# A hybrid decoder step: token scales of the first blocks taken from rows, dt's projection in small PSUM tiles, a second weight tile that lags, and a passage whose scalings are asked for in four parts

## The chip, the core and the metric

The kernel runs on one core of a Trainium2 chip: TensorE (PE; its weight loads are PEld), VectorE (DVE), ScalarE (ACT), GpSimd (POOL) and SyncE (SP), which here only starts DMAs. Each engine runs its own list of instructions in order; semaphores join them. The metric is the device time of one execution in microseconds (us). Before the change it was 2792.21 us, the median of three runs (2789.77 to 2793.71).

## The reference, cut to what matters

A trunk of two layers runs over 1104 token rows: 64 sample tokens, 16 learned meta tokens and 1024 prompt tokens, of 1024 features each. Layer 0 is a Mamba-2 mixer and a feed-forward block, layer 1 a sliding-window attention and a feed-forward block. The change touches only the way into layer 0:

```python
def _rmsnorm(x, g):
    xf = x.astype(jnp.float32)
    r = lax.rsqrt(jnp.mean(xf * xf, axis=-1, keepdims=True) + EPS)
    return (xf * r).astype(x.dtype) * g

def _mamba2_mixer(u, ...):              # u = _rmsnorm(h, ssm_norm_g)
    zxbcdt = u @ w_in                   # 2048 z, 3072 x/B/C, 32 dt columns
    z, xbc, dt_raw = ...
    ...                                 # conv of 4 taps over xbc, silu
    dt = jax.nn.softplus(dt_raw + dt_bias)
    a = dt * (-jnp.exp(a_log))
    y, h_new = _ssd_chunked(...)        # chunks of 128 tokens
    out = _gated_group_rmsnorm(y + xs * d_skip, z, gate_g) @ w_out
```

So each token needs one scale, the root of its mean square, before any column of `w_in` can be applied to it.

## The kernel before

Tokens stand in two halves: 592 (the 64 sample and 16 meta tokens, the block of 80, and four blocks of 128) and 512 (four blocks of 128). In SBUF the features lie on the partitions: `hA` holds the first half as 8 feature tiles of 128 by 592. A product keeps float32 accuracy by three passes of a faster format: weight and token operands are split into a high and a low part (`wH`, `wL`, `uH`, `uL`), and each 128-feature tile takes wH·uH, wH·uL and wL·uH (lines L75 to L77 in `mm3`). ScalarE casts the high part (L138 for weights), VectorE or GpSimd subtracts to get the low part (L149). `ws` holds a raw weight as it was loaded, 128 by 1024; both parts are then stored to DRAM (`kept`, L152) for the second half. Only two buffers each of `ws`, `wH` and `wL` exist.

**The opening** is `input_first`, written out by hand for the first two weight tiles (B and C of group 0). The first half is cut at token 336 (`at[0]`, `at[1]`): the first part is blocks 0 to 2, the second blocks 3 and 4. For the first part the square of each feature tile is taken (L345, L347), and one-column matmuls against ones add it over the features (L350), so the sums come out with tokens on the partitions. `roots` is one power on GpSimd (L356), `diagonal` writes the scales on a diagonal (L361), and `spread` multiplies it by ones (L368), which puts each token's scale on all partitions. Then `scaled` (L372), `high` (L375) and `low` (L378) make the operands tile by tile, and `dense` (L385) runs the products, both weight tiles for each feature tile. For blocks 3 and 4 rows of tokens are loaded instead, and ScalarE squares and sums each in one instruction (L403). `warm` (L337) runs matmuls of ones whose result is not used. `in_order` chains the instructions of this part on TensorE, VectorE, ScalarE and GpSimd in the order of the list.

After it, `xbc` projects the other tiles of group 0; `conv` (L647 to L668) reads each accumulator out of PSUM with two ScalarE copies and runs the taps on VectorE (`cc`, L664). `dt_proj` (L485) is the projection to dt in full float32, from the unscaled tokens, with the gain folded into its weight `wdt` by GpSimd (L436); its result is copied to `dtraw` (L490), and the token's scale is applied later in `dt_tables`. `acc` names the large accumulators of PSUM (two in the first half, three in the second), `ps` the small ones (four and five). A group's `ssd` takes a chunk at a time; group by group the sample tokens are decoded (`decode`, matmul L811, operand `decs`), and each chunk needs a table of decays, `E`, broadcast from DRAM by SP (L601).

**The passage** (`boundary`) joins the halves: the last out-projections of the first half run while `input_second` reads, scales (L471) and splits the second half's tokens. A string of letters gives the order of the parts, and `in_order` holds it on TensorE.

Outside these places the program's own scheduler sets the order on every engine, by priorities and its own idea of times, before the program runs.

## Time and profile before

| | |
|---|---|
| median of three runs | 2792.21 us |
| the profiled execution | 2798.55 us, its span 2796.7 us |
| mean granted TensorE clock | 0.985 |
| TensorE busy | 2723.8 us (97%) |
| VectorE, ScalarE, GpSimd busy | 1988.1, 1193.6, 525.2 us |
| first product matmul (L385) | at 17.13 us |
| first matmul after the opening (L75) | at 38.06 us |

In rows in order of time, the first number is the start in us, the second the busy time; `out<-in` are the program's tiles, `xN` is the count of instructions, and the bracket holds how long the engine was idle before and what ended that. A matmul's time includes its way through the array, so neighbours overlap; the distance of two starts is the cost of one. The granted clock is the share of TensorE's full clock that it was given.

### The profile page before, as it was taken

What the parts mean: (1) busy time and instruction counts of PE and PEld (TensorE: products, weight loads), DVE (VectorE), ACT (ScalarE), POOL (GpSimd) and SP (SyncE); (2) the same over time, 40 slices, a digit from 0 to 9 for tenths busy, and PEclk for the clock granted to TensorE, in tenths of its full rate; (3) what the DMA queues carried; (4) which work ended last, traced back from release to release, by engine and by line L of the source; (5) the groups of instructions that cost most, each with busy time, mean ns of one, the idle gap of its engine ahead of it and who ended that gap; (6) DMA issues with size and microseconds to landing.
All of it is one profiled execution on the core that took longest, in us unless ns stands there. A gap on an engine that the chain in (4) does not pass through costs nothing.

```text
span 2796.7 us, 50176 instructions
## 1 busy us (share of the span) xinstructions
PE 2723.8 (97%) x19649; PEld 2515.4 (90%) x19649; DVE 1988.1 (71%) x3401; ACT 1193.6 (43%) x2491; POOL 525.2 (19%) x740
## 2 busy tenths in 40 slices
PE   9899999999999999999999999999999999999998
PEld 8788999887888899999999997676989999999998
DVE  7677666666564898778779881556479777877886
ACT  4656554356441443334342142555444333334224
POOL 2565545315322100000000002433220000000000
PEclk9999999999999999999999999999999999999999
DMA  7766767566554344334378652011714443438764
GB/s 267 246 218 218 270 225 246 210 232 203 190 189 155 121 145 164 139 123 166 130 291 286 235 190 81 27 44 29 215 59 153 153 142 122 166 136 293 275 217 160
DMA packets 261713, 498.60 MB, mean 178 GB/s; under 512 B 23652, under 2 KB 140004, under 8 KB 261476
## 3 DMA queue, kind: packets, MB, share of 16 engines
q1 hardware_dynamic: 257748, 488.49, 50.9%
q10 hardware_dynamic: 3728, 6.90, 0.7%
q8 instruction: 155, 2.54, 0.4%
q14 instruction: 82, 0.67, 0.1%
HBM read 320.01 MB, written 175.30 MB: 177 GB/s over the span
## 4 chain that ended last, share of the span: by engine, by line
PE 84%; DVE 8%; ACT 2%; DMA 2%; issue 1%; POOL 1%; SPq 0%; POOLq 0%; DVEq 0%; ACTq 0%
PE wacc L1589 10%; PE wacc L1591 10%; PE wacc L1590 10%; PE acc L75 6%; PE acc L76 6%; PE acc L77 6%; PE dacc L1589 5%; PE dacc L1590 5%; PE dacc L1591 5%; PE pP L75 2%; PE pP L76 2%; PE pP L77 2%; PE ps L746 1%; PE ps L749 1%; DVE cc L664 1%
## 5 line engine op out<-in xcount | busy, mean ns | idle before, releaser
L1245 ACT CAST wo<-ws 128x512 fp32r<-128x512 f32 x428 | 263.3, 620 | 537.6 <-PE wacc L1590 250.3
L1589 PE MATMUL dacc<-bo,wo 128*128 128x276 f32 (+1 forms) x1232 | 355.5, 289 | 4.8 <-ACT sumX L1777 2.1
L1590 PE MATMUL dacc<-bo,wo 128*128 128x276 f32 (+1 forms) x1232 | 356.0, 289 | 0.0
L1591 PE MATMUL dacc<-bo,wo 128*128 128x276 f32 (+1 forms) x1232 | 355.2, 289 | 0.0
L1246 DVE TENSOR_TENSOR wo<-ws,wo 128x512 fp32r<-128x512 f32 x428 | 296.3, 696 | 49.6 <-ACT wo L1245 38.7
L75 PE MATMUL acc<-uH,wH 128*128 128x336 f32 (+2 forms) x808 | 267.6, 331 | 2.6 <-ACT wH L138 2.2
L77 PE MATMUL acc<-uH,wL 128*128 128x336 f32 (+2 forms) x808 | 266.4, 330 | 1.2 <-DVE wL L149 1.2
L76 PE MATMUL acc<-uL,wH 128*128 128x336 f32 (+2 forms) x808 | 266.6, 330 | 0.0
L1589 PEld LDWEIGHTS dacc<-bo,wo 128*128 128x128 f32 x1232 | 232.6, 189 | 5.6 <-ACT sumX L1777 2.3
L1590 PEld LDWEIGHTS dacc<-bo,wo 128*128 128x128 f32 x1232 | 231.9, 188 | 0.0
L1591 PEld LDWEIGHTS dacc<-bo,wo 128*128 128x128 f32 x1232 | 231.8, 188 | 0.0
L75 PEld LDWEIGHTS acc<-uH,wH 128*128 128x128 f32 x808 | 154.1, 191 | 18.2 <-issue 4.9
L77 PEld LDWEIGHTS acc<-uH,wL 128*128 128x128 f32 x808 | 153.7, 190 | 13.2 <-issue 3.1
L76 PEld LDWEIGHTS acc<-uL,wH 128*128 128x128 f32 x808 | 153.6, 190 | 12.5 <-issue 3.9
L664 DVE SCALAR_TENSOR_TENSOR cc<-raw,vectors_sb,cc 128x616 f32<-128x616 f32 (+1 forms) x144 | 135.1, 945 | 41.1 <-ACT cc L662 39.5
L2442 POOL MEMSET mask<- 128x64 f32 x1 | 0.2, 151 | 715.0 <-PE dacc L1591 715.0
L75 PE MATMUL acc<-yH,wH 128*128 128x336 f32 (+1 forms) x360 | 122.9, 342 | 9.2 <-DVE hA L917 3.7
L77 PE MATMUL acc<-yH,wL 128*128 128x336 f32 (+1 forms) x360 | 121.0, 336 | 0.5 <-DMA wL<-kept 0.5
L76 PE MATMUL acc<-yL,wH 128*128 128x336 f32 (+1 forms) x360 | 120.9, 336 | 0.5 <-DVE yL L82 0.5
L1765 DVE TENSOR_TENSOR hN<-hN,dacc 128x552 f32<-128x552 f32 (+1 forms) x132 | 94.3, 718 | 19.8 <-PE dacc L1591 19.2
L1589 PE MATMUL wacc<-N4H,wo 128*128 128x276 f32 (+1 forms) x352 | 103.0, 293 | 5.3 <-DVE hA L1602 2.4
L1589 PE MATMUL wacc<-B11H,wo 128*128 128x276 f32 (+1 forms) x352 | 103.4, 294 | 3.0 <-DVE big L917 3.0
(569 smaller groups left out, 8502.7 us busy)
## 6 DMA issues: line engine op xcount, KB each, us to landing
kept<-wH SPq DMA_DIRECT2D x56, 512.0 KB, 3.2
kept<-wL SPq DMA_DIRECT2D x56, 512.0 KB, 3.4
ws<-ffn_w_gate SPq DMA_DIRECT2D x44, 512.0 KB, 4.1
ws<-ffn_w_up SPq DMA_DIRECT2D x44, 512.0 KB, 4.5
ws<-ffn_w_down SPq DMA_DIRECT2D x44, 512.0 KB, 5.8
ws<-ssm_w_in SPq DMA_DIRECT2D x40, 512.0 KB, 5.2
wH<-kept SPq DMA_DIRECT2D x38, 512.0 KB, 3.4
wL<-kept SPq DMA_DIRECT2D x38, 512.0 KB, 4.4
```

Source lines behind the costliest of these rows:

```text
L75: nc.tensor.matmul(out, wH, xH, start=start, stop=False)
L76: nc.tensor.matmul(out, wH, xL, start=False, stop=False)
L77: nc.tensor.matmul(out, wL, xH, start=False, stop=stop)
L664: nc.vector.scalar_tensor_tensor(o, raw[:, k : k + n], w(k), o, ALU.mult, ALU.add)
L746: nc.tensor.matmul(pyv[64 * q : 64 * q + 64, t, :], xd[:n, t, q, :], Ev[:, 4 * q + t, :], start=True, stop=True)
L749: nc.tensor.matmul(pst[:], bt[lo:n], xw[lo:n].rearrange("p t q d -> p (t q d)"), start=True, stop=True)
L1245: nc.scalar.copy(H, src)
L1246: (low or nc.vector).tensor_tensor(L, src, H.bitcast(F32), ALU.subtract)
L1589: nc.tensor.matmul(out, wH, xH, start=start, stop=False, skip_group_check=True)
L1590: nc.tensor.matmul(out, wH, xL, start=False, stop=False, skip_group_check=True)
L1591: nc.tensor.matmul(out, wL, xH, start=False, stop=stop, skip_group_check=True)
L1765: add = lambda d, s: nc.vector.tensor_tensor(d, d, s, ALU.add)
```

## The change

Four edits. (1) All five blocks of the first half are now loaded as rows too, the first three ahead of the turned tokens; ScalarE squares and sums each (`squares`). The one-column matmuls and the squares by feature tile go. The vectors and the identity are loaded from ScalarE's queue. The first weight is loaded between the second and third token load, the second after the last. `warm` now reads the second row block in place of the ones. (2) `dt_proj` writes one small PSUM tile for each part of the tokens instead of one large accumulator, and copies each. (3) In the opening's products the second weight tile follows two feature tiles behind the first; its high half is cast inside the loop. (4) `input_second` yields after each second feature tile, and the passage's string asks for the four parts between out-projections.

```diff
-    K.load_ident = lambda: nc.sync.dma_start(cst[:, :128], I["cmask"][:, :128])
+    K.load_ident = lambda: nc.scalar.dma_start(cst[:, :128], I["cmask"][:, :128])
-    nc.sync.dma_start(small[:], I["vectors"])
+    nc.scalar.dma_start(small[:], I["vectors"])
@@ input_first
-        for q, k in ((nc.sync, 0), (nc.scalar, 4), (nc.sync, 2), (nc.sync, 6)):
-            load(q, 0, slice(k, k + 2))
-        for w in W.queue[:2]:
-            W._load(w)
         load_vectors(K, I, self.hp)
         K.load_ident()
+        rows = [self.quad("xr") for _ in range(3)]
+        for c in range(3):
+            nc.sync.dma_start(rows[c][: blocks[c][1]], I["token_rows"][slice(*np.cumsum(blocks[c]))])
+        order = [lambda k=k: load(nc.sync, 0, slice(k, k + 2)) for k in (0, 2, 4, 6)]
+        order.insert(2, lambda: W._load(W.queue[0]))
+        for x0 in order:
+            x0()
+        W._load(W.queue[1])
+        rows += [self.quad("xr") for _ in range(2)]
+        for c in range(3, 5):
+            nc.sync.dma_start(rows[c][:], I["token_rows"][slice(*np.cumsum(blocks[c]))])
...
+        def squares(c):
+            n = blocks[c][1]
+            nc.scalar.activation(rows[c][:n], rows[c][:n], AF.Square, accum_out=v[:n, c : c + 1])
...
-        warm(3)
-        sums(As)
+        for c in As:
+            squares(c)
+        warm(rows[1], 3)
         roots(A)
         diagonal(As)
-        warm(1)
         ra = spread(0, As)
-        for t in range(2):
-            ws[t] = W._split_high(W.queue[t])
+        ws[0] = W._split_high(W.queue[0])
...
+        def two(t, k):
+            if 0 <= k < KD:
                 dense(t, 0, k, 0, self.uH, start=k == 0)
                 dense(t, 0, k, 0, self.uL)
+        for k in range(KD + 2):
+            if k < KD:
+                high(0, k)
+                if k == 1:
+                    ws[1] = W._split_high(W.queue[1])
+                if k in (4, 6):
+                    squares(1 + k // 2)
+                if k + 2 < KD:
+                    scaled(0, k + 2, ra)
+                low(0, k)
+            two(0, k)
+            two(1, k - 2)
+        roots(B)
...
+            three(0, k)
+            three(1, k - 2)
@@ input_second
-        yield
+            if k % 2:
+                yield
@@ dt_proj
-        ps = self.acc()
+        self.dtraw = self.tmp("dtraw")
         for a, b in chunks(H):
+            ps = self.ps()
...
-        self.dtraw = self.tmp("dtraw")
-        nc.scalar.copy(self.dtraw[:, : H["n"]], ps[:, H["base"] : H["base"] + H["n"]])
+            nc.scalar.copy(self.dtraw[:, a:b], ps[:, : b - a])
@@ boundary
-        for x in "xloonoooroooywwbwwwwww":
+        for x in "xloonoooroooywwbwbwbwbwww":
```

The program that this gives, at three places. First TensorE at the turn from the first to the second part of the tokens (`dg` is the diagonal of scales, `hA` the tokens, `wdt` dt's weight). Before:

```order
L385 MATMUL acc<-uH_91,wL 128x336 x4
L385 MATMUL acc<-uH_92,wL 128x336 x4
L368 MATMUL ps<-dg,one 128x128 x2
L385 MATMUL acc<-uH_91,wL 128x336 x4
L385 MATMUL acc<-uH_92,wL 128x336 x4
L385 MATMUL acc<-uH_91,wH 128x256
```

and now:

```order
L378 MATMUL acc<-uH_91,wL 128x336 x4
L378 MATMUL acc<-uH_92,wL 128x336 x4
L361 MATMUL ps<-dg,one 128x128
L490 MATMUL ps<-hA,wdt 32x336 x6
L361 MATMUL ps<-dg,one 128x128
L490 MATMUL ps<-hA,wdt 32x336 x2
L490 MATMUL ps<-hA,wdt 32x256 x3
L378 MATMUL acc<-uH_91,wL 128x336 x4
L378 MATMUL acc<-uH_92,wL 128x336 x4
L490 MATMUL ps<-hA,wdt 32x256 x5
L378 MATMUL acc<-uH_91,wH 128x256
```

The sixteen matmuls of dt's projection, which stood behind the whole second part, now stand ahead of it, six of them between the two matmuls of the second spread.

Second, ScalarE in the opening (`xr,xv<-xr` is a square of a row block, `uH<-sq` the cast of a scaled feature tile). Before:

```order
L345 ACTIVATE sq<-hA 128x336 x4
L138 CAST wH<-ws 128x1024 x2
L375 CAST uH_91<-sq 128x336 x3
L403 ACTIVATE xr,xv<-xr 128x1024
L375 CAST uH_91<-sq 128x336
L375 CAST uH_92<-sq 128x336
L403 ACTIVATE xr,xv<-xr 128x1024
L375 CAST uH_92<-sq 128x336 x3
```

and now:

```order
L345 ACTIVATE xr,xv<-xr 80x1024
L345 ACTIVATE xr,xv<-xr 128x1024 x2
L138 CAST wH<-ws 128x1024
L368 CAST uH_91<-sq 128x336 x2
L138 CAST wH<-ws 128x1024
L368 CAST uH_91<-sq 128x336 x2
L368 CAST uH_92<-sq 128x336
L345 ACTIVATE xr,xv<-xr 128x1024
L368 CAST uH_92<-sq 128x336 x2
L345 ACTIVATE xr,xv<-xr 128x1024
L368 CAST uH_92<-sq 128x336
```

The cast of the second weight moved in between the casts of the tokens, and the two squares of blocks 3 and 4 stand two casts later each, the second ahead of the last cast alone.

Third, VectorE in the passage (`sq<-big` is a scaling, `hA<-hA,acc` a residual add). Before:

```order
L471 SCALAR_TENSOR_TENSOR sq<-big,vectors_sb,rb 128x512 x4
L82 TENSOR_TENSOR uL_5869<-sq,uH_5867 128x512
L917 TENSOR_TENSOR hA<-hA,acc 128x592
L82 TENSOR_TENSOR uL_5869<-sq,uH_5867 128x512 x2
L471 SCALAR_TENSOR_TENSOR sq<-big,vectors_sb,rb 128x512
L82 TENSOR_TENSOR uL_5869<-sq,uH_5867 128x512
L471 SCALAR_TENSOR_TENSOR sq<-big,vectors_sb,rb 128x512
```

and now:

```order
L474 SCALAR_TENSOR_TENSOR sq<-big,vectors_sb,rb 128x512 x4
L82 TENSOR_TENSOR uL_5842<-sq,uH_5840 128x512
L921 TENSOR_TENSOR hA<-hA,acc 128x592
L82 TENSOR_TENSOR uL_5842<-sq,uH_5840 128x512 x2
L474 SCALAR_TENSOR_TENSOR sq<-big,vectors_sb,rb 128x512
L82 TENSOR_TENSOR uL_5842<-sq,uH_5840 128x512
L474 SCALAR_TENSOR_TENSOR sq<-big,vectors_sb,rb 128x512
```

Apart from line and buffer numbers nothing moved there, on this or any other engine. Between the opening and the first out-projection of group 0 the scheduler has set another order on all engines: the first matmul of group 1's decode (L811) has 63 more projection matmuls ahead of it than before, and on SP the third to fifth load of a decay table (L601, `E`) have one more weight load and two or three more stores of weights ahead of them. In the feed-forward and attention stages some neighbours change places.

More of the change, by code (lines that the diff above doesn't have):

```diff
@@ L422, in input_first, with three @@
                     scaled(1, k, rb)
-        for k in range(KD):
-            high(1, k)
-            if k + 2 < KD:
-                scaled(1, k + 2, rb)
-            low(1, k)
-            for t in range(2):
+        def three(t, k):
+            if 0 <= k < KD:
                 dense(t, 1, k, 0, self.uH, start=k == 0)
@@ L431, in input_first @@
                 dense(t, 1, k, 1, self.uH, stop=k == KD - 1)
+        for k in range(KD + 2):
+            if k < KD:
+                high(1, k)
+                if k + 2 < KD:
+                    scaled(1, k + 2, rb)
+                low(1, k)
+            three(0, k)
+            three(1, k - 2)
         self.rooted = [x for x in traced[begin:] if x.engine == nc.gpsimd.engine]
@@ L2670, in tokens @@
     turned = lambda a: np.ascontiguousarray(a.reshape(-1, KD, 128).transpose(2, 1, 0))
[L2671 to L2672 removed]
+    return {"token_rows": np.ascontiguousarray(x), "tokens_a": turned(x[:cut]), "tokens_b": turned(x[cut:end]), "tokens_c": turned(x[end:])}
 def device_shape(n, shape):
```

41 lines of the change are left out of this document (5 added, 36 removed).

## Prediction

> **What bounds the kernel now.** I read the profile from the outside in: the engines' shares of the whole span, then the stages that the change can reach, then the first 45 us in order of time. The first line is the page's row of busy times; the five below it give busy us of each engine (with instructions), granted TensorE clock, DMA share and GB/s from one time to another.
>
> ```profile
> PE 2723.8 (97%) x19649; PEld 2515.4 (90%) x19649; DVE 1988.1 (71%) x3401; ACT 1193.6 (43%) x2491; POOL 525.2 (19%) x740
> ...
> 0.00:17.13 17.13, 14.44 (x63) 9.77 (x63) 4.67 (x14) 5.93 (x10) 1.58 (x14) 0.82 0.92 322
> 17.13:38.06 20.93, 18.67 (x132) 16.44 (x133) 16.65 (x38) 12.19 (x27) 5.53 (x9) 0.90 0.73 263
> 38.06:110.00 71.94, 64.56 (x473) 61.16 (x470) 52.69 (x88) 44.96 (x103) 35.90 (x65) 0.95 0.64 225
> 110.00:265.00 155.00, 146.31 (x1099) 128.13 (x1099) 124.85 (x170) 98.26 (x245) 91.93 (x107) 0.95 0.69 233
> 265.00:550.00 285.00, 277.31 (x2079) 258.06 (x2079) 187.29 (x258) 132.33 (x263) 134.23 (x134) 0.99 0.67 236
> ```
>
> TensorE sets the span: it idles 73 us of 2796.7. The change cannot touch the dense work; it can only move when that work begins (17.13, after 63 matmuls that feed no product), shorten the ragged stretch to 38.06, and alter the 16 us of idle time between 38 and 265, since a new opening also gives other engine orders there. Beyond 265 little is left. The opening in order of time (start, us, engine, line):
>
> ```profile
> 6.73 5.96 PE L350 MATMUL ps<-one,sq 128*80 128x1 f32 x48
> 6.85 0.48 ACT L345 ACTIVATE sq<-hA 128x336 f32<-128x336 f32 x1 [0.45 <-DMA hA<-tokens_a]
> 8.15 1.05 ACT L138 CAST wH<-ws 128x1024 fp32r<-128x1024 f32 x1 [0.81 <-DMA ws<-ssm_w_in]
> 9.45 1.04 ACT L138 CAST wH<-ws 128x1024 fp32r<-128x1024 f32 x1 [0.26 <-DMA ws<-ssm_w_in]
> 13.04 0.85 POOL L356 TENSOR_TENSOR xr<-xv,xe 128x3 f32<-128x3 f32 x1 [11.79 <-DVE xv L353]
> 13.93 0.65 DVE L361 TENSOR_SCALAR dg<-cmask_sb,xr 80x80 f32<-80x80 f32 x3 [1.04 <-POOL xr L356]
> 14.40 1.49 PE L368 MATMUL ps<-dg,one 80*128 80x80 f32 x6
> 16.01 1.51 DVE L372 SCALAR_TENSOR_TENSOR sq<-hA,vectors_sb,ps 128x336 f32<-128x336 f32 x3 [1.43 <-issue]
> 17.13 0.65 PE L385 MATMUL acc<-uH,wH 128*128 128x336 f32 x1 [1.24 <-ACT uH L375]
> 23.23 1.22 DVE L149 TENSOR_TENSOR wL<-ws,wH 128x1024 fp32r<-128x1024 f32 x1
> 24.50 1.50 PE L385 MATMUL acc<-uH,wL 128*128 128x336 f32 x8
> 27.03 1.25 DVE L372 SCALAR_TENSOR_TENSOR sq<-hA,vectors_sb,ps 128x256 f32<-128x256 f32 x3
> 28.49 0.28 PE L385 MATMUL acc<-uH,wH 128*128 128x256 f32 x1
> ...
> 34.16 0.28 PE L385 MATMUL acc<-uL,wH 128*128 128x256 f32 x1
> 34.17 1.05 ACT L138 CAST wH<-ws 128x1024 fp32r<-128x1024 f32 x1 [1.68 <-issue]
> 35.12 0.59 ACT L647 COPY raw<-acc 128x528 f32<-128x528 f32 x1
> 35.61 0.22 ACT L648 COPY raw<-acc 128x64 f32<-128x64 f32 x1
> 35.93 2.20 PE L485 MATMUL acc<-hA,wdt 128*32 128x336 f32 x32 [1.37 <-ACT raw L648]
> 38.06 0.42 PE L75 MATMUL acc<-uH,wH 128*128 128x336 f32 x1
> 38.22 5.02 DVE L664 SCALAR_TENSOR_TENSOR cc<-raw,vectors_sb,cc 128x616 f32<-128x616 f32 x5 [1.75 <-ACT cc L662]
> ```
>
> The weights' high halves lie ready at 10.5; the first scaling at 16.01 waits only for the token scales, which come through the 48 one-column sums until 12.7. From 16.01 to 23.23 VectorE is continuous, and TensorE follows it. Between 34.3 and 38.06 TensorE does 2.2 us of dt's projection and waits 1.37 for an accumulator.
>
> **The change part by part.** Its further rows: the idle matmuls, a square of a token block, the second root, dt's gain, three casts, and the clock before and after its rise.
>
> ```profile
> 1.45 5.49 PE L337 MATMUL ps<-one 128*128 128x512 f32 x6 [1.45 <-DVE one L329]
> 16.60 1.42 ACT L375 CAST uH<-sq 128x336 fp32r<-128x336 f32 x3 [6.11 <-DVE sq L372]
> 17.93 1.05 ACT L403 ACTIVATE xr<-xr 128x1024 f32<-128x1024 f32 x1
> 18.89 0.18 ACT L403 ACTIVATION_READ_ACCUMULATOR xr<-xr 128x1 f32 x1
> 22.63 2.38 POOL L356 TENSOR_TENSOR xr<-xv,xe 128x2 f32<-128x2 f32 x1 [8.73 <-DMA big<-state_ssm]
> 24.98 0.61 POOL L436 TENSOR_TENSOR wdt<-wdt,vectors_sb 128x256 f32<-128x256 f32 x1
> 18.00:21.40 3.40, 3.40 (x12) 3.40 (x13) 3.40 (x8) 3.40 (x9) 0.00 (x0) 0.52 1.00 339
> 21.40:24.80 3.40, 3.40 (x23) 3.13 (x22) 3.05 (x7) 0.68 (x2) 2.17 (x1) 1.00 0.84 308
> ```
>
> *Scales from rows.* Before, 1344 KB of tokens had landed by 6.85 and each weight of 512 KB took 1.30 us more. The three row blocks are 1344 KB too; with 156 KB of vectors and identity on ScalarE's queue beside them the third lands at about 7.25 and the second at 5.95. A square costs 1.05 + 0.18, so the third is done at 8.5; the root 0.85 and about 0.25 for the mean and two hand-overs, the diagonal 0.65: 10.25. The idle matmuls now read the second block after its square, so they start at 7.2, and the spread stands behind them. Six passes took 5.49 (to 12.7); with the clock up after 3.4 us of them they end at 11.65. I take 12.2. The spread took 1.6 (14.40 to 16.01): first scaling 13.8, a **lead of 2.2**. The tokens, now behind the rows, land 3.8 us later, the first at about 8.5 and the last at 12 (the order in which they alternate with the first weight included), and the second weight at 13.3: in time, and so hidden, as long as the idle matmuls end last.
>
> *ScalarE in that stage.* It now casts the second weight there (1.05) and squares two more blocks (1.05 each until the next cast starts), among eight casts of 0.47: 6.95 us from 14.4, to 21.35; the last low half 0.5 later, 21.85. VectorE alone would be done 2.2 us early, but the last cast stands behind the second square, so the low half of the first weight starts **1.4 earlier** than 23.23. The root of the second blocks runs beside that split as now, and the second scaling starts at 25.6.
>
> *dt's projection.* Sixteen matmuls of 0.14 us leave the place at 35.93 and fill TensorE's pauses between the two low-weight groups. Six stand ahead of the second spread and wait for the gain (25.59 now, 24.2 then): done at 25.0, the spread at 25.3, before VectorE wants it. The other ten delay the dense second part: 25.3 + 0.7 + 1.25 (eight low-weight matmuls) + 0.7 gives 27.95, and its 48 matmuls, 5.8 us as now, end at 33.7, only 0.6 earlier. But dt is then paid. Its accumulator is no longer asked for, so the 1.37 us go.
>
> *The lag.* The first tile's last nine matmuls come ahead of the end: it ends 1.1 us early, at 32.6. ScalarE's cast of the next weight (1.05) and the first raw copy (0.71) follow: 34.4. TensorE starts the next tile there, and waits some 0.3 for VectorE's low half of the weight: **3.3 earlier** than 38.06. ScalarE then copies the second tile (0.7) and casts (1.06) before the first conv: VectorE's chain starts at 37.15, only **1.1 earlier** than 38.22. Between these two ends I take 2.3: TensorE is the busier in 38 to 110 (64.56 against 52.69 us), while the decay tables come through VectorE.
>
> *Passage and second half.* VectorE's scalings there, and dt's second projection with the next accumulation after it:
>
> ```profile
> 528.86 3.93 DVE L471 SCALAR_TENSOR_TENSOR sq<-big,vectors_sb,rb 128x512 f32<-128x512 f32 x4
> 551.62 1.92 PE L485 MATMUL acc<-big,wdt 128*32 128x512 f32 x16
> 551.72 0.77 DVE L917 TENSOR_TENSOR hA<-hA,acc 128x592 f32<-128x592 f32 x1 [2.93 <-PE acc L77]
> ```
>
> The four yields change the list, but not what the scheduler emits: the engine orders of the passage are row for row those of before, four scalings first and then single ones among the residual adds. Its price is 0; a gain would need the same order to run faster. dt's second projection keeps its place and may, in its new bank, have to wait for the last residual add at 551.72 (up to 0.9); its copy is behind by then. I take 0, since it waits for VectorE in both programs.
>
> *The order of 60 to 265.* The decode matmuls and the decay tables' loads get other places:
>
> ```profile
> PE ps L811 <- DVE decs L781: 3.9, 1, 3.9
> ...
> 80.42 0.70 PE L557 MATMUL ps<-tot,cmask_sb 64*128 64x256 f32 x2 [2.19 <-POOL tot L553]
> ...
>   DMA E<-acsd: 13.9, 5
> ```
>
> The first row is TensorE's longest wait, in group 1's decode at 175; the second its wait for GpSimd's part of dt's tables; the third ScalarE's idle time, five waits for decay tables. In the new order 63 more projection matmuls stand ahead of that decode matmul (31 of 336 columns and 32 of 256; the 48 from 28.49 took 0.12 each at 256 columns, so 0.155 at 336: 8.6 us), against a lead of 3.3 and, ahead of its operand on VectorE, one more weight split of 1.22 and three more gate steps. That removes between nothing and the 3.9. Other pieces lose: I take 1.0.
>
> **The sum.** 2.3 + 1.0 = 3.3. The profiled execution took 2798.55 (1.85 around its span) and becomes 2795.2; the median shown, 6.3 below it, becomes 2788.9.
>
> **The rivals.**
>
> *The decode's wait goes whole.* TensorE keeps 3.3 and loses the 3.9: 7.2, 2785.0. For it speaks that TensorE is the bound before and after; against it that VectorE ran 125 of the 155 us there.
>
> *The lead is given back.* VectorE's and GpSimd's chain through dt's tables gains 1.1 only, dt's bank takes up to 0.9: 2792.0. For it: at 80.42 TensorE already waits 2.19 for that chain.
>
> *The clock comes one slot later.* TensorE now does nothing until 7.2 and then pauses at 13; the product starts at half rate, as it did before. In 3.4 us TensorE did 12 matmuls at clock 0.52 and 23 at 1.00, 0.135 us more for each; one more such slot costs 1.6, of the lead: 2790.5. The Trainium skill, page TensorE: Matmul & The Clock Gate, Part 1, speaks against removing early TensorE work in the same way: half rate is the default, and a full busy window of about 3.4 us that runs freely is needed to leave it. By that rule alone the time is that of this rival.
>
> *Slower: the decay tables' loads.* SP issues in order. In the new order the third to fifth of these loads stand behind one more weight load and two or three more stores, and such a load waits for the projection ahead of it: one tile is 24 matmuls of 0.155 and 24 of 0.12, 6.6 us. Where the table then lands last, the chunk is 6.6 late, less the lead of 2.3, plus half a slot of lost clock in the longer pause (1.7): 6.0 slower, 2798.2. It decides from the point where the 13.9 us of those five waits grow by more than the lead. Against it: the weights themselves come earlier.
>
> **How the numbers follow.** Chances: forecast 0.50 (2788.9, its own range 2786 to 2792), decode's wait 0.24, lead given back 0.13, clock 0.05, decay loads 0.08. A measurement of this kernel tells 0.2%, 5.6 us, from no change: faster is below 2786.6, slower above 2797.8. Faster takes the 0.24 and 0.04 of the forecast's lower edge, slower the last rival's 0.08, and 0.64 remains. The range reaches from just below the first rival to just under the slow one, 2784 to 2797.
>
> **What would show it.** First scaling at 13 to 14.5 us; the second tile's last matmul near 33.7 and the next tile's first near 34.5, with dt's matmuls between 24 and 28; VectorE's first conv near 37; the passage's rows 3 us earlier and spaced as before; TensorE's idle time between 38 and 265 within 3 us of 16. Wrong would be: a first scaling set by a token landing, a second spread that waits for dt, ScalarE's waits for decay tables above 18 us, or a passage that is shorter.

## The result, and the profile after

The changed kernel takes **2775.05 us** (median of 9 runs, 2768.29 to 2784.12); beside it the kernel before took 2793.16 (9 runs, 2785.84 to 2796.21). The ratio is **0.9938, 95% interval 0.9923 to 0.9952**: some 17 us faster (0.62% of 2793; from 13 to 22 by the interval). The forecast was 2788.9, with 2784.0 as the lower end of its range: the change gained about five times what I had summed up. Its profiled execution took 2775.05, with a span of 2773.0.

The page's row of busy times, after:

```profile
PE 2706.8 (98%) x19599; PEld 2502.0 (90%) x19599; DVE 1990.4 (72%) x3395; ACT 1195.2 (43%) x2494; POOL 526.6 (19%) x740
```

The five stretches that the prediction showed of before, with the same columns (stretch, its length, busy us of PE, PEld, DVE, ACT and POOL, granted clock, DMA share, GB/s):

```profile
0.00:17.13 17.13, 7.45 (x20) 3.92 (x21) 5.63 (x15) 9.61 (x16) 1.65 (x14) 1.00 0.93 334
17.13:38.06 20.93, 19.85 (x138) 15.19 (x137) 13.63 (x31) 9.86 (x23) 4.18 (x11) 1.00 0.88 315
38.06:110.00 71.94, 67.81 (x507) 65.10 (x507) 55.10 (x91) 45.78 (x105) 39.50 (x65) 0.98 0.70 239
110.00:265.00 155.00, 147.12 (x1163) 131.65 (x1162) 133.04 (x176) 102.38 (x254) 99.07 (x111) 0.98 0.71 246
265.00:550.00 285.00, 276.94 (x2040) 255.20 (x2039) 185.00 (x254) 129.32 (x259) 130.34 (x132) 0.99 0.68 239
```

In 38 to 110 TensorE now does 507 matmuls instead of 473, and in 110 to 265 1163 instead of 1099. All three other engines are busier in the second of these stretches (VectorE 133.04 us against 124.85). The clock is 0.98 in both, against 0.95. So the gain stands less in the opening than behind it. The 1.00 in the first row needs care: the profile of after has no clock record ahead of 11.12 us (that of before none ahead of 7.60), and a stretch without one is shown as 1.00. The opening itself in order of time:

```profile
7.44 4.66 PE L341 MATMUL ps<-xr,one 128*128 128x512 f32 x6 [7.44 <-ACT xr L345]
...
12.80 1.51 DVE L365 SCALAR_TENSOR_TENSOR sq<-hA,vectors_sb,ps 128x336 f32<-128x336 f32 x3 [2.08 <-PE ps L361]
13.93 0.42 PE L378 MATMUL acc<-uH,wH 128*128 128x336 f32 x1 [1.16 <-ACT uH L368]
...
21.33 1.22 DVE L149 TENSOR_TENSOR wL<-ws,wH 128x1024 fp32r<-128x1024 f32 x1
...
24.28 1.32 PE L490 MATMUL ps<-hA,wdt 128*32 128x336 f32 x12
25.54 0.49 PE L361 MATMUL ps<-dg,one 128*128 128x128 f32 x2
25.95 1.19 PE L490 MATMUL ps<-hA,wdt 128*32 128x336 f32 x10
26.06 1.27 DVE L365 SCALAR_TENSOR_TENSOR sq<-hA,vectors_sb,ps 128x256 f32<-128x256 f32 x3 [0.86 <-PE ps L361]
28.50 1.05 PE L490 MATMUL ps<-hA,wdt 128*32 128x256 f32 x10
29.48 0.38 PE L378 MATMUL acc<-uH,wH 128*128 128x256 f32 x1
...
34.33 1.05 ACT L138 CAST wH<-ws 128x1024 fp32r<-128x1024 f32 x1 [2.80 <-DMA ws<-ssm_w_in]
35.16 0.28 PE L378 MATMUL acc<-uH,wL 128*128 128x256 f32 x1
36.05 0.42 PE L75 MATMUL acc<-uH,wH 128*128 128x336 f32 x1 [0.60 <-ACT raw L652]
38.38 3.77 DVE L668 SCALAR_TENSOR_TENSOR cc<-raw,vectors_sb,cc 128x616 f32<-128x616 f32 x3 [1.75 <-ACT cc L666]
```

The product begins 3.2 us earlier (13.93 against 17.13), the second tile ends 1.0 later than before (35.16 against 34.16, since dt's records now stand ahead of its second part), and the next tile starts 2.0 earlier (36.05 against 38.06). (A matmul in full float32 leaves two records, so dt's 16 matmuls are 32.) VectorE's chain starts 0.16 later (38.38 against 38.22).

TensorE's waits, by what ended them (us in all, times, longest): before, from 30 to 552 us, two that the prediction did not show:

```profile
PE acc L75 <- ACT wH L138: 2.2, 1, 2.2
PE ps L811 <- POOL decB L784: 1.8, 1, 1.8
```

and after, from 30 to 540:

```profile
PE acc L75 <- DVE th L841: 5.1, 1, 5.1
PE acc L75 <- DVE hA L921: 3.5, 1, 3.5
```

Both of the decode's waits (3.9 and 1.8) are gone, the one for the weight's cast (2.2) has shrunk to 0.9, and one of 5.1 us for the gate's `th` is new.

By stages, from the starts of the same matmuls in the trace of each kernel's one profiled execution (us): "first half" is from 38.0 to the first product of the second half, so a lead at 38 is in it; then up to the first of the feed-forward's first products, to the first of its down products, to the first product of the attention stage, to its last projection, and to the end. Each ratio is to the kernel before as it ran beside that kernel, and is not the quotient of two medians of the table.

| kernel | median (runs) | ratio to before, 95% | first half | second half | feed-forward up | down | attention | last feed-forward |
|---|---|---|---|---|---|---|---|---|
| before | 2793.16 (9) | | 527.2 | 380.3 | 483.4 | 238.9 | 337.9 | 791.0 |
| after | 2775.05 (9) | 0.9938 [0.9923, 0.9952] | 513.7 | 375.6 | 485.4 | 236.4 | 336.4 | 787.5 |
| before, passage alone | 2793.41 (11) | 1.0012 [1.0001, 1.0023] | 528.1 | 380.2 | 482.2 | 239.8 | 333.8 | 790.4 |
| before, dt alone | 2778.88 (5) | 0.9955 [0.9941, 0.9968] | 514.0 | 377.5 | 481.7 | 240.4 | 337.8 | 789.8 |
| after, opening alone | 2790.31 (11) | 0.9990 [0.9978, 1.0003] | 522.5 | 379.4 | 482.2 | 240.1 | 333.2 | 793.1 |
| after, no lag | 2777.24 (5) | 0.9947 [0.9933, 0.9960] | 515.5 | 376.0 | 483.5 | 239.9 | 333.3 | 790.6 |
| after, dt held back | 2784.50 (11) | 0.9968 [0.9955, 0.9980] | 527.6 | 377.7 | 481.0 | 236.5 | 336.5 | 791.9 |

The two profiled spans differ by 23.7 us: 13.5 in the first half, 4.7 in the second, 2.5 in the down products, 2.0 lost ahead of them, and 5.0 in the last two stages. The profiled execution of before lies 5.4 above the median of its nine, so that much of the 23.7 is that execution's and not the change's. The last two stages are not the change's either: the attention stage takes 333 to 334 or 336 to 338 in kernels of both kinds, 333.8 in the passage alone, which is the kernel before instruction for instruction, and the last stage varies by 6 us in the table without regard to kind. The first half is steadier: 527.2 and 528.1 for that one order.

### The profile page after: what moved, and what is told of

It reads as the page before. It is cut to its first block, busy times and chain, and to the rows that moved or that the text cites. A ratio compares the mean times of both kernels' runs of the same rounds, so it can differ in the third digit from the quotient of the medians.

```text
span 2773.0 us, 50074 instructions
## 1 busy us (share of the span) xinstructions
PE 2706.8 (98%) x19599; PEld 2502.0 (90%) x19599; DVE 1990.4 (72%) x3395; ACT 1195.2 (43%) x2494; POOL 526.6 (19%) x740
## 5 line engine op out<-in xcount | busy, mean ns | idle before, releaser
L75 PE MATMUL acc<-uH,wH 128*128 128x336 f32 (+2 forms) x808 | 267.4, 331 | 7.1 <-DVE th L841 5.1
L77 PE MATMUL acc<-uH,wL 128*128 128x336 f32 (+2 forms) x808 | 266.3, 330 | 1.3 <-POOL wL L149 1.2
L75 PEld LDWEIGHTS acc<-uH,wH 128*128 128x128 f32 x808 | 153.9, 190 | 21.4 <-DVE th L841 5.3
L76 PEld LDWEIGHTS acc<-uL,wH 128*128 128x128 f32 x808 | 153.6, 190 | 13.9 <-issue 5.3
L77 PEld LDWEIGHTS acc<-uH,wL 128*128 128x128 f32 x808 | 153.5, 190 | 13.4 <-issue 3.2
L75 PE MATMUL acc<-yH,wH 128*128 128x336 f32 (+1 forms) x360 | 121.8, 339 | 6.9 <-DVE hA L921 3.5
L77 PE MATMUL acc<-yH,wL 128*128 128x336 f32 (+1 forms) x360 | 119.7, 332 | 0.5 <-DMA wL<-kept 0.5
L1593 PE MATMUL wacc<-T2H,wo 128*128 128x276 f32 (+1 forms) x352 | 102.2, 292 | 3.8 <-ACT T2H L81 3.8
```

The source lines that it names most:

```text
L75: nc.tensor.matmul(out, wH, xH, start=start, stop=False)
L76: nc.tensor.matmul(out, wH, xL, start=False, stop=False)
L77: nc.tensor.matmul(out, wL, xH, start=False, stop=stop)
L1593: nc.tensor.matmul(out, wH, xH, start=start, stop=False, skip_group_check=True)
```

## The experiments

The prediction's theory was: some 2 us from the opening, about 1 from the new order behind it, nothing else. Against it stood, after the result, that the change set a **better order of all engines from 60 to 290 us**, through one of its parts; that **one wait** or one stall was what went; that the **half-rate stretches** of the clock were; and that the **passage** gave something after all.

### Which part

*dt's small tiles alone*, put into the kernel before:

```diff
-        ps = self.acc()
+        self.dtraw = self.tmp("dtraw")
         for a, b in chunks(H):
+            ps = self.ps()
...
-                        ps[32 * q : 32 * q + 32, H["base"] + a : H["base"] + b], self.wdt[:, f, :], ...
+                        ps[32 * q : 32 * q + 32, : b - a], self.wdt[:, f, :], ...
...
-        nc.scalar.copy(self.dtraw[:, : H["n"]], ps[:, H["base"] : H["base"] + H["n"]])
+            nc.scalar.copy(self.dtraw[:, a:b], ps[:, : b - a])
```

> The kernel before with one part of the change alone: dt's projection in small PSUM tiles (opening, lag and passage as before). VectorE's order between 38 and 265 us is then row for row that of the changed kernel. Theory 'order' (the new places of work between 38 and 265, above all the group-1 decode matmul that no longer waits 3.9 us, carry the gain): this kernel takes two thirds of the 18 us, 2781 (2778 to 2785), TensorE's idle time between 38 and 265 falls from 16 to below 13. Theory 'opening' (earlier scales, and a product that starts at full clock, carry it): 2790 to 2793, since only the 1.4 us wait for an accumulator and some of dt's 2.2 us go. Theory 'clock' (neither; what differs is how many 3.4 us slots TensorE gets at half rate): the time follows the granted clock of each execution, 2.8 us for each 0.001, and at equal clock this kernel stands within 3 us of the kernel before.

*The opening alone*: the changed kernel with dt in its accumulator at the end of the opening (the lines above the other way round), and the passage as before.

> The other half: the changed kernel with dt's projection as before (one accumulator, at the end of the opening) and the passage as before; rows, ScalarE's squares and the lag stay. The order between 38 and 265 is then nearly that of the kernel before. Theory 'order': 2787 to 2790, only the opening's 2 to 4 us are won, and the decode matmul of group 1 waits 3 to 4 us again. Theory 'opening': 2777 to 2781. Theory 'clock': time and granted clock move together, with no difference left at equal clock.

*Without the second tile's lag*: the changed kernel with the two loops as in the kernel before.

```diff
-            two(0, k)
-            two(1, k - 2)
+            if k >= 1:
+                for t in range(2):
+                    for kk in ([0, 1] if k == 1 else [k]):
+                        dense(t, 0, kk, 0, self.uH, start=kk == 0)
+                        dense(t, 0, kk, 0, self.uL)
```

> The changed kernel without the lag of the second tile: both tiles' matmuls of a piece stand together again, as in the kernel before; all else stays, and the order between 38 and 265 is that of the changed kernel. In the feed-forward and attention stages the order differs from the changed kernel's in some 90 rows of VectorE. By the prediction's step the lag is worth 1.1 us at the end of tile 0: 2776 (2774 to 2779), with the first out-projection 0 to 1.5 us later than in the changed kernel. Rival: the 10 us that the changed kernel's profiled execution gains behind 551 us come from the other order there; then this kernel lies 4 to 8 us above the changed one, 2779 to 2783, with that loss behind 900 us.

*The passage alone*, in the kernel before:

```diff
-        yield
+            if k % 2:
+                yield
...
-        for x in "xloonoooroooywwbwwwwww":
+        for x in "xloonoooroooywwbwbwbwbwww":
```

> The kernel before with the passage's four yields and its new string alone. The order of every engine is row for row that of the kernel before, so this is also a measure of what two timings of one instruction stream differ by: 2793 within 3 us, ratio 0.999 to 1.001. The rival, a passage that is worth something by itself, would show as 2 us or more with the rows around 530 to 552 us spaced otherwise.

The four ran on one chip, with 2791.91 for the kernel before. dt's tiles alone give 2778.88 (0.9955), nearly the whole gain. The new opening alone gives 2790.31 (0.9990, which does not exclude no gain at all); its next tile starts at 36.15, 1.9 earlier, as in the changed kernel. Without the lag the result is 2777.24 (0.9947), not to be told from the changed kernel's 0.9938. The passage alone has, on every engine, the order of the kernel before row for row; its 1.0012 [1.0001, 1.0023] is therefore a comparison of a program with itself, and says that these intervals do not tell differences of 0.1%. So one part, dt's, made 12 to 13 of the 17 us.

To see where, I cut the first half at the 240th, the 880th and the 1192nd matmul of the projection (lines L75 to L77): between these stand as many matmuls in all of these kernels. Before, with the same columns as above:

```profile
71.77:231.79 160.02, 147.38 (x1097) 128.33 (x1096) 115.87 (x166) 104.86 (x264) 94.95 (x123) 0.95 0.70 238
231.79:291.00 59.21, 55.78 (x417) 52.65 (x416) 45.00 (x54) 31.97 (x69) 29.20 (x31) 0.94 0.62 210
```

after:

```profile
70.11:221.64 151.53, 141.38 (x1098) 126.05 (x1096) 121.17 (x170) 104.02 (x263) 98.37 (x123) 0.97 0.74 252
221.64:276.28 54.64, 52.78 (x417) 49.83 (x416) 43.37 (x53) 32.48 (x70) 27.38 (x31) 1.00 0.64 223
```

dt's tiles alone:

```profile
72.14:222.04 149.90, 139.87 (x1098) 125.06 (x1096) 121.20 (x170) 103.89 (x263) 97.69 (x123) 0.98 0.74 254
```

the opening alone:

```profile
69.87:228.82 158.95, 147.93 (x1097) 129.39 (x1096) 114.49 (x165) 104.08 (x263) 97.53 (x123) 0.94 0.71 239
```

In the first of these pieces 160.0 and 159.0 us without dt's part, 151.5 and 149.9 with it; in the second 59.2 before and 54.6 after. TensorE idles 12.6 of the 160.0 and 10.2 of the 151.5 us; at clocks of 0.95 and 0.97 it loses 8.0 and 4.5; some 2.5 of the 8.5 are longer records of its matmuls, for which I have no row. VectorE packs 121.2 us of work into 151.5 (80%) instead of 115.9 into 160.0 (72%); such a share rises by itself when a stage gets shorter, so it describes the gain and does not explain it.

The clock of the executions does not explain it either: at equal mean clock 6 to 13 us remain. At mean clocks of 0.987, 0.988 and 0.989 the executions of the kernel before have medians of 2791.9, 2790.5 and 2788.4 us (30 in all); the changed kernel took 2782.4, 2784.1 and 2779.4 there (one each), and dt's tiles alone 2781.2 and 2777.4 at the first two (two each).

### dt's place or its bank

In the changed kernel dt's matmuls are held behind the last one of the opening's product, and keep their small tiles:

```diff
         self.rooted = [...]
+        self.lastmm = [x for x in traced[begin:] if x.engine == nc.tensor.engine][-1]
...
+                    n0 = len(traced)
                     self.dt_proj(hf)
+                    in_order(tc, [self.lastmm] + traced[n0:], nc.tensor)
```

> The changed kernel with one thing put back: dt's 16 matmuls keep their small PSUM tiles but are held behind the opening's dense product, where they stood before. The order between 38 and 265 us then falls back nearly to that of the kernel before (its first decode matmul behind 480 projection matmuls, not 507). Theory 'place' (dt done early lets the scheduler give the later order, and that order carries the gain): this kernel loses it again, 2787 to 2791. Theory 'bank' (an accumulator that dt no longer takes carries it, whatever the order): 2775 to 2779.

It took 2784.50 (0.9968), and its first piece is as long as before:

```profile
69.90:229.45 159.55, 148.06 (x1098) 129.37 (x1096) 112.99 (x170) 104.58 (x263) 96.27 (x122) 0.95 0.69 236
```

So the gain of the first half hangs on where dt stands, not on its bank: with dt behind the opening the scheduler returns nearly to the old order (480 projection matmuls ahead of group 0's first decode matmul, the opening's 96 counted in, as before; 507 in the changed kernel). The time says less: by the ratio some 9 of the 17 us are left, between what the two theories gave. In this profile the second half is 2.6 and the down products 2.4 us shorter than before, and the opening alone makes 2.8 by its ratio: added up, as an estimate, 7.8. That its median is 5.8 below the opening alone stays open: the spans of the two profiles differ by 0.8 only, but the profiled execution here (2791.06) lies 6.6 above the median of its kernel.

### One wait, one stall, one slow stretch

*Group 1's decode two steps later*, in the kernel before, so that the 3.9 us of `decs` are covered by projection matmuls:

```diff
             yield
+            for _ in range(2 if g == 1 else 0):
+                yield
             yield from self.decode(g, st[0])
```

> The kernel before, with only the decode of group 1 emitted two steps later. TensorE then has 79 more projection matmuls ahead of that group's first decode matmul (831 of them instead of 752; the changed kernel has 815), and group 0 stays as it was. If the 3.9 us wait for the decode's operand, with the two half-rate slots behind it (6.8 us, 3.4 us lost), is the main piece of the new order, this kernel gains 5 to 8 us: 2784 to 2787, with no wait of over 1 us at that line behind 150 us. If the gain is spread over all of the new order, it gains 0 to 3: 2789 to 2792.

831 projection matmuls stand ahead of that decode now instead of 752 (815 in the changed kernel), and its wait for `decs` is gone. The time is 2798.60, 1.0015 [1.0004, 1.0026]: nothing gained. TensorE's waits from 72 to 292 us are led by another, which was 2.2 before:

```profile
PE acc L75 <- ACT wH L138: 6.4, 2, 3.6
```

*The stalled multiply.* One VectorE multiply of 80x640 took 5.03 us before at 251, 4.54 after at 166, and 0.81 or 0.82 elsewhere. After, with the GpSimd work beside it:

```profile
165.82 1.89 POOL L788 TENSOR_TENSOR decB<-decx,cmask_sb 96x1024 fp32r<-96x1024 f32 x1 [1.55 <-DVE decx L785]
166.38 4.54 DVE L728 TENSOR_TENSOR big<-big,cb 80x640 f32<-80x640 f32 x1
167.67 1.18 POOL L725 TENSOR_TENSOR xw<-xd,twdec 80x256 f32<-80x256 f32 x2
168.81 1.43 POOL L854 TENSOR_TENSOR sq<-sq,th 128x592 f32<-128x592 f32 x1
```

It ends at 170.92, 0.7 after a train of GpSimd work that began ahead of it. In both kernels its second operand was left in PSUM instead, where it costs no extra work (group 2 before, group 1 after):

```diff
         nc.scalar.copy(bt[:n], pb[:n, 0:128])
+        if first and g == 2:
+            cb = pb[:, 128:256]
```

> The kernel before with one operand moved: the masked 80x80 product of group 2's first chunk stays in PSUM, and VectorE's multiplication of 80x640 elements that took 5.03 us at 251 us (0.81 and 0.82 in groups 0 and 1) reads it there instead of from SBUF. No engine's order changes. Theory 'contention' (VectorE with two SBUF inputs waits for GpSimd's running instructions): it takes 0.8 to 1.0 us, TensorE's wait of 3.19 us at 260 falls below 0.5, the two half-rate slots behind it go, and the time is 4 to 6 us shorter: 2786 to 2788. Rival: the multiplication waits for an operand and is as long as before; 2792.

> The changed kernel with the same move in group 1, where the multiplication took 4.54 us at 166 us (0.81 and 0.82 in groups 0 and 2) and TensorE then waited 5.12 us for VectorE at 171.65. No engine's order changes. Theory 'contention': 0.8 to 1.0 us for the multiplication, a wait below 1.7 us at 168 to 172, one half-rate slot less, and 4 to 6 us shorter: 2769 to 2771, which would beat both kernels. Rival: GpSimd's work (decode's table and the square sums, to 170.2) ends as late as now and something else waits for it: 2774 to 2776.

In the kernel before, the multiply and the VectorE instruction behind it became:

```profile
250.71 0.81 DVE L726 TENSOR_TENSOR big<-big,ps 80x640 f32<-80x640 f32 x1
251.44 4.27 DVE L664 SCALAR_TENSOR_TENSOR cc<-raw,vectors_sb,cc 128x616 f32<-128x616 f32 x1
```

The stall went to the next instruction with two operands in SBUF. In the changed kernel the multiply took 0.80 too, and TensorE's 5.1 us for `th` fell to 1.3. But from 160 to 200 us two other waits now stand beside it, which the changed kernel does not have there:

```profile
PE ps L817 <- DVE big L818: 2.8, 2, 2.3
PE acc L75 <- DVE th L843: 1.3, 1, 1.3
PE ps L817 <- DVE decs L787: 1.3, 1, 1.3
```

The times are 2791.52 (0.9994 [0.9983, 1.0005]) and 2775.16 (0.9930 [0.9917, 0.9944], against 0.9938): no gain in either.

*A filled pause.* Fourteen idle matmuls of 512 columns stand ahead of group 1's first decode matmul, in the kernel before, where TensorE waits and the clock falls:

```diff
                 ps = self.ps()
+                for _ in range(14 if g == 1 and b == 0 else 0):
+                    nc.tensor.matmul(ps[:], XB[:, 0, 0], XB[:, 0].rearrange("p c m -> p (c m)"), start=True, stop=True)
```

> The kernel before with 14 idle matmuls of 512 columns put on TensorE right ahead of group 1's first decode matmul, where it waits 3.91 us at 175 us. They read the decode's own table (ready at 171.8), write the bank that the decode matmul then overwrites, and fill some 3 us of the wait; what is waited for stays as late. So the computed work and the waits are those of the kernel before, and only TensorE's pause is filled. Theory 'clock' (a slot that TensorE leaves more than half empty is followed by one or two slots at half rate): the two half-rate slots of 174.9 to 181.7 are gone, the next projection matmuls run at full rate, and 2 to 3.4 us are saved: 2789 to 2791. Theory 'pause' (the wait itself is the whole price): the slots stay or their going saves nothing; 2793 to 2794.

The wait and the 6.29 us behind it, before:

```profile
171.20:175.31 4.11, 0.20 (x2) 0.03 (x1) 2.81 (x3) 2.82 (x5) 1.98 (x2) 0.94 0.18 64
175.31:181.60 6.29, 6.29 (x35) 5.25 (x36) 4.44 (x6) 3.55 (x7) 2.89 (x2) 0.50 0.55 176
```

and with the fill:

```profile
169.50:173.71 4.21, 3.68 (x16) 2.58 (x15) 2.90 (x3) 2.85 (x5) 2.07 (x2) 1.00 0.26 89
173.71:180.00 6.29, 6.29 (x55) 5.79 (x56) 5.28 (x8) 5.15 (x9) 2.89 (x2) 1.00 0.52 175
```

The fill does its work on the spot: full clock, 55 matmuls instead of 35 in the same 6.29 us. At the 880th projection matmul this is given back, 159.4 us from the 240th against 160.0, and the time is 2797.79 (1.0010 [0.9996, 1.0024]). The half-rate stretch behind that wait was thus slack: something else than TensorE sets the pace of these 160 us.

*The wait in front of 34.33.* In the changed kernel the row at 34.33 says that ScalarE's cast of the next weight waited 2.80 us for its load. Three decode-state loads were held behind the sixth weight on SyncE's queue, so that the weight came earlier:

```diff
             nc.sync.dma_start(h0, rows(self.I["state_ssm"], j))
+            if g == 0 and j < 3:
+                in_order(self.tc, [self.W.loads[5], nc.cur_bb.bb.instructions[-1]], nc.sync)
```

> The changed kernel with SyncE's order alone edited: the three loads of decode states (512 KB each, issued from 19.6 us, first read at 86 us) are held behind the sixth weight. ScalarE's cast of the third weight waited 2.80 us for its landing until 34.33, and VectorE's split and first conv came behind it. TensorE's and VectorE's orders do not change. Theory 'opening counts': cast at 31.5 to 32.5, the first conv on VectorE at 36 to 37 instead of 38.4, the next tile's first matmul at 34 to 35.5 instead of 36.05, and 1 to 2.5 us less at the end: 2772.5 to 2774. Theory 'given back': the lead shows in the first 40 us and is gone by 225 us, where TensorE waits for VectorE and ScalarE anyway: 2775 within 1.5.

```profile
33.96 1.05 ACT L139 CAST wH<-ws 128x1024 fp32r<-128x1024 f32 x1 [2.79 <-issue]
```

The cast starts 0.37 earlier, not 2.8, and it still waits 2.79, now without a load at its end. By its place, just behind the last matmul that reads the older of two such buffers, the buffer held it; that was read from the trace and not tried. The next tile starts at 35.67 (36.05 without it), and the time is 2774.83 (0.9928 [0.9906, 0.9949]): the same.

*The passage in its written order* on VectorE, in the changed kernel:

```diff
+            if i == 13:
+                late = len(traced)
             next(part[x])
...
+        in_order(self.tc, [x for x in traced[late:] if x not in self.W.lows], self.nc.vector)
```

> The changed kernel with VectorE made to keep the passage's written order: two scalings with their low halves, then a residual add, and so on, instead of four scalings first. (In the changed kernel the scheduler undoes that order, and TensorE waits 3.53 us at 526.7 for a residual add.) If the written order is what the passage needs: that wait falls below 1 us, the half-rate slot behind it goes, and the time is 3 to 5 us shorter, 2770 to 2772. If VectorE is the bound there in any order: the wait comes back at another residual add or at the second half's first product, and it stays at 2774 to 2776.

TensorE's waits for the residual adds from 515 to 545 us, 3.5 in one wait without it, became

```profile
PE acc L75 <- DVE hA L922: 6.7, 4, 3.0
```

and the time 2779.09 (0.9953 [0.9935, 0.9970] against 0.9938; not told apart). The order in which the change writes the scalings is no hidden gain.

### Which place in the order

In the new order ScalarE begins group 0's decode behind the eleventh cast of a weight, in the old one behind the tenth. In the kernel before, I put it there; then group 1's as well, behind the eighteenth; and in the changed kernel back ahead of the eleventh:

```diff
+                    for g, n in ((0, 10),):
+                        in_order(tc, [self.W.casts[n], self.heads[g]], nc.scalar)
```

(`(0, 10), (1, 17)` for the second; the two ends of the list exchanged for the third.)

> The kernel before with one more order on ScalarE: the decode of group 0 begins behind the eleventh weight cast instead of the tenth. Opening, dt and passage stay. TensorE then has 508 projection matmuls ahead of its first decode matmul (480 before, 507 in the changed kernel), and the rest of the stage is ordered anew behind it. Theory 'start of the decode' (this one place is what dt's early end changes, and it carries the stage): projection matmul 880 comes 7 to 10 us earlier than in the kernel before, and the time is 2780 to 2785. Theory 'whole order' (several places together): 0 to 4 us, 2789 to 2793.

> As the last, and group 1's decode also behind the eighteenth cast (the seventeenth comes ahead of it in the kernel before's next order; the changed kernel has 17 and 18): TensorE has 508 and 830 projection matmuls ahead of the two decodes, 507 and 815 in the changed kernel. Theory 'start of the decode': 2778 to 2783, 1 to 3 us better than with group 0 alone. Theory 'whole order': within 3 us of the kernel before.

> The reverse: the changed kernel with one order on ScalarE put back, the decode of group 0 ahead of the eleventh weight cast. TensorE has 482 projection matmuls ahead of its first decode matmul, and 769 ahead of group 1's (480 and 752 in the kernel before). dt stays early and in small tiles, the opening stays. Theory 'start of the decode': 7 to 10 us are lost, 2783 to 2787 (some 3 of them may be the feed-forward stage's order, which changes too). Theory 'bank and early dt' (what dt frees carries the gain): 2775 to 2778.

Group 0's decode later, in the kernel before: 2787.55 (0.9975 [0.9962, 0.9988]). Both later: 2783.98 (0.9964 [0.9950, 0.9978]). Group 0's earlier, in the changed kernel: 2787.15 (0.9972 [0.9961, 0.9982], against 0.9938). By the ratios, group 0's decode behind 28 more projection matmuls (508 ahead of its first instead of 480) thus makes about 7 of the 17 us in the one direction (5.4 by the medians), and putting it back costs some 9 in the other; there the feed-forward's order changed as well, so the second number is not the decode's alone. None of the three times falls within a range put down for it: the last two lie 1 us and less beyond that of 'start of the decode', the first between the two theories. Group 0's decode later, in the kernel before, in both pieces:

```profile
71.80:225.06 153.26, 141.09 (x1097) 126.46 (x1096) 115.31 (x166) 103.17 (x262) 97.78 (x123) 0.96 0.71 249
225.06:278.57 53.51, 52.91 (x418) 49.77 (x416) 42.63 (x53) 32.93 (x71) 32.44 (x31) 1.00 0.62 225
```

and back ahead, in the changed kernel, the first piece:

```profile
70.44:225.23 154.79, 147.03 (x1097) 128.66 (x1096) 116.90 (x170) 104.70 (x263) 94.78 (x122) 0.96 0.72 243
```

The first pieces lie between 160.0 and 151.5. With the second one, the decode's later place alone makes the stretch 206.8 us, as short as in the changed kernel (206.2; 219.2 before), and the whole first half 516.2, 11.0 shorter than before; put back, the changed kernel's first half is 521.6 instead of 513.7. With both groups' decodes later, in the kernel before, the two pieces are

```profile
71.85:220.54 148.69, 136.27 (x1093) 123.66 (x1092) 116.36 (x162) 99.76 (x251) 92.08 (x120) 0.95 0.73 251
220.54:280.39 59.85, 55.98 (x422) 52.18 (x421) 44.93 (x58) 36.38 (x82) 30.38 (x35) 0.97 0.65 219
```

the first as short as in the changed kernel, the second as long as before. So this one place carries most of what the order is worth in the first half: 11.0 us put in and 7.9 taken out, of 11.5. What it lacks of the changed kernel is elsewhere: its second half is 381.1, against 375.6, and it has no lead from the opening. That its time gains only 5 to 7 us and not 11 stays open; its profile has nothing longer than before but the second half (0.8), the down products (1.0) and the last stage (2.2). Why the scheduler sets this order when dt is early was not taken apart further, nor why the stage runs faster in it. One thing goes with it in the traces: ScalarE's waits for decay tables (`E`), 13.9 us in five waits in the prediction's row, are in the changed kernel, from 60 to 265 us,

```profile
ACT E L707 <- DMA E<-acsd: 4.9, 3, 3.5
```

From 60 to 300 us they come to 13.9 before, 14.6 with dt held back, 10.2 in the opening alone and 9.5 with the decode put back; 6.1 with group 0's decode later, 5.3 with dt's tiles alone and 4.9 after. Whether they set the pace of the stage or only follow it was not tried.

## Why the prediction was wrong, point by point

**Opening: right in size.** It took 2.3 for it: the next tile starts 2.0 earlier, the opening alone measures 0.9990, and beside dt's part alone the whole change is 3.8 us faster by the medians (intervals overlap). That the size fits is in part luck: inside, errors of both signs met. The idle matmuls end at 12.10 (12.2 predicted), but the first scaling starts at 12.80, not 13.8: the spread took 0.87 us (11.93 to 12.80) at full clock, where I had taken over the 1.6 that it needed at half. The first weight's low half is at 21.33 (21.85). The second spread, which was not to be late, stood behind dt's first 12 records (24.28 to 25.60), so that the second scaling is at 26.06 (25.6); the other 20 records took 2.2 us in two places, and the second tile's end came out at 35.16 instead of 33.7. The lead of 3.3 on TensorE shrank to 2.0 there and at the cast of the next weight, which I had at 32.6 and which starts at 34.33; VectorE's lead of 1.1 is 0.16 us behind.

**The order of 60 to 265: the failed step.** I took 1.0, between nothing and the 3.9 of one wait. The change is worth 11.5 us between the next tile's start and the second half (13.5 less the 2.0 of the lead, in one profile each), and 13.1 of it between the 240th and the 1192nd projection matmul, less 1.6 lost around them. Three things were wrong in the working of it. The bound of 3.9 counted a single wait, while TensorE's loss there was 12.6 us idle and 8.0 in half-rate clock over 160 us. It took that wait as the thing to be saved, but covering it (the decode two steps later) gave nothing, and filling it gave nothing either; both times the gain was lost again within 120 us, so something else paces that stage. And it priced a new order by the neighbours of one matmul. What the runs showed in its place: the first half's gain is the order that dt's early end leads to, and most of it (in the profiles 11.0 us put in, 7.9 taken out) hangs on one step of ScalarE's order, the decode of group 0 behind one more cast. What paces the stage in either order stays open. TensorE's idle time between 38 and 265 us, which was to stay within 3 us of 16, came out at 12.0. The 63 matmuls that I had counted ahead of group 1's decode were the sign of it in the order; I read them as cover for one wait.

**dt's small tiles: mis-sized with it.** I costed dt as 2.2 us moved and 1.37 freed. Put in alone they made 12 to 13 us, by the order that dt's early place led to.

**"Beyond 265 little is left": wrong by about 5.** The second half is 4.7 us shorter in the profile, and 2.6 to 4.7 in every kernel of the table with dt in small tiles (0.9 in the opening alone, 0.1 in the passage alone); the down products are 2.4 to 2.5 shorter in two of them. TensorE's waits before, from 565 to 947 us:

```profile
PE wacc L1589 <- DVE big L917: 3.0, 1, 3.0
PE acc L75 <- DMA wH<-kept: 2.6, 1, 2.6
```

After, from 551 to 929:

```profile
PE acc L75 <- DVE sum L1231: 1.8, 1, 1.8
PE wacc L1593 <- DVE big L921: 0.6, 1, 0.6
```

In the down products before, from 1428 to 1668:

```profile
PE dacc L1589 <- ACT sumX L1777: 2.1, 1, 2.1
PE dacc L1589 <- DVE big L1618: 1.2, 1, 1.2
```

where only 0.8 us for `big` are left after. I had noted that some neighbours change places there, and priced none.

**The passage and dt's second projection: right.** Price 0: the order is that of before, and alone it gives nothing. Its rows come 13 to 15 us earlier, not 3, and are not closer together (from the first scaling to dt's second projection 23.8 us, 514.33 to 538.16; before 22.8, 528.86 to 551.62).

**The rivals.** The decode's wait did go whole, as the first had it, at a place where that was worth nothing by itself. Of the lead of 2.0, 1.7 is left at the 240th projection matmul. The clock did not come late: it stands at 1.00 from 11.1 us to 38, so the product starts at full rate, at 13.93; before, it stood at half from 11.0 to 21.3. The idle passes did run at half rate first: they start 0.85 us apart from 8.46 to 11.02, the last 0.49 behind, and the next record 0.43 behind that, so the clock rose some 3.6 us after the first of them. I had taken 3.4. The rule that I had cited for that rival (the Trainium skill, TensorE: Matmul & The Clock Gate, Part 1: a full busy window of about 3.4 us to leave half rate) agrees with that. But the slot that I took to be lost was lost before the change, to the 48 one-column sums (below). The slow rival has the wrong sign: ScalarE's waits for decay tables shrank by 9.0 us instead of growing.

## What to carry to other kernels

Where a scheduler sets the order, price an edit by the stage whose order it changes and by that stage's whole loss (idle time, slow clock, and how densely the second busiest engine is packed), not by the longest wait in it: a wait, a stall and a pause taken away singly here gave nothing, while the order that came with one early projection gave over 10 us. Test such an edit alone before crediting the large one that it came with; here the small PSUM tiles alone made 12 to 13 of the 17 us, and the rebuilt opening about 3. And run one comparison of a program with itself: here it came out at 1.0012 with an interval that excludes 1, which sets the size below which nothing is to be read.

## What was new about the hardware

**The clock follows the busy share of the slot before, and not sharply.** In the traces the granted clock changes in slots of 3.413 us, whose grid lies differently in every execution. Over the sixteen profiles of this case, from 40 to 2700 us, taking slots at full clock, by TensorE's busy share in the slot and what the next slot got:

```
busy share    next slot at half
below 0.30       55 of 55
0.30 to 0.45     68 of 69
0.45 to 0.55     24 of 51
0.55 to 0.65      7 of 75
0.65 to 0.80      6 of 198
0.80 to 0.95      2 of 303
0.95 and more    22 of 11480
```

The Trainium skill (TensorE: Matmul & The Clock Gate, Part 1) has the free-running window of that length; it agrees. The last row's 22 lie in stretches with small matmuls (of 1 or 32 columns, or of 64 or 80 rows). The opening shows it too: before, the 48 one-column sums fill the record from 6.73 to 12.7, and the clock stands at half from 11.0 to 21.3. So a record that is busy throughout did not keep the clock up there. An execution's time goes with its granted clock: the changed kernel took 2768.29 at a mean of 0.993 and 2784.12 at 0.988, about 3 us for each 0.001; over the executions of the kernel before it is half of that (medians of 2797.1 at 0.983 and 2788.4 at 0.989). That the grid's phase is what differs between them was not tried.

**GpSimd can hold up one VectorE instruction five times its length.** 0.81 us became 4.54 beside four GpSimd operations in a row, and 0.80 with one operand in PSUM. The Trainium skill (SBUF — State Buffer, SBUF: two separate sides) has an exclusive lock on the ports that the two share: of a VectorE operation with two inputs in SBUF and a GpSimd operation that reads SBUF, the first to start holds it for its whole instruction. The runs agree with it, and add that VectorE here came in only behind the whole train (170.24), not behind the first of its operations (167.71), and that the stall passes to the next such operation (4.27).

**The name at the end of a wait is the last to come, not always the cause.** A wait put down to a load (2.80) stayed 2.79 when the load came earlier.
